# 64 keys by 64 queries in a half of TensorE's columns, in place of 128 by 128, for a gated recurrence's products

## The chip, the core and the metric

The kernel runs on one core of a Trainium2 chip. The metric is the device time of one execution in microseconds (us). The engines are TensorE (PE, with its weight loads, PEld, shown apart), VectorE (DVE), ScalarE (ACT), GpSimd (POOL) and SyncE (SP), which here only issues DMAs.

## What is computed

One layer of a decoder trunk for 256 tokens of width 2048, in fp32. A normalised input is multiplied by a wide matrix (12288 columns); its columns feed a short convolution (branch A), a gated linear recurrence (branch B) and merge gates. Both branches are projected back, merged and added, and a second gated term and a last normalisation follow. The change lies in branch B:

```python
def step(state, inp):
    qn, kn, vn, fn = inp
    b = jnp.cumsum(fn, axis=2)
    ...
    diff = b[:, :, :, None, :] - b[:, :, None, :, :]
    decay = jnp.exp(jnp.where(causal, diff, 0.0)) * causal_f
    a = jnp.einsum('bhtk,bhtsk,bhsk->bhts', qn, decay, kn)
    o = inter + jnp.einsum('bhts,bhsv->bhtv', a, vn)
```

Each of 8 heads has 128 features. `a[t, s]` couples a query at token t with a key at an earlier token s, and the decay between the two depends on the feature, so it can't be taken out of the sum over features as one factor per pair of tokens.

## The kernel before

The 256 tokens are held as two blocks of 128; the second is stored in reverse order, so that both blocks meet at their last rows. Products with weight matrices run in `product` (L859 to L864): each fp32 weight chunk and each activation is split into a high and a low part (float32r; `split`, L113 to L128, makes `whi` on ACT at L124 and `wlo` on DVE at L125), and three products per tile (high by high, high by low, low by high) are summed in PSUM banks named `g`. The main loop (L867 to L943) takes one weight chunk of 256 rows by 512 columns per step: 12 records of 512 columns on PE. Chunks are split three steps ahead (`LEAD`, L149), with four buffers for each part.

The work that follows each product is a generator: the main loop calls `advance()` once per step, and each generator then issues its work up to its next `yield`. So the order of each engine's instructions is fixed by the program: a generator's work is laid between the projections' products, a piece per step.

The recurrence is `hgrn(j)` (L341 to L514), run for j = 0 and 1, four heads each, called from `ep_og` (L333). It forms the 128 by 128 matrix a of each block and head without a loop over tokens:

- For each level size B in 128, 64, 32, 16, 8, 4 (`LEVELS`, L31), tokens of the later half of a group of B are coupled with those of its earlier half. The decay of such a pair factors at the boundary between the halves, so `level(B)` (L393) scales keys and queries with exponentials into a tile X, for which DVE and POOL each do two of the four parts (`combine`, L378), and `products(X)` (L355) multiplies for each head all 128 keys with all 128 queries. Of the first block X takes the keys of the earlier halves and the queries of the later ones, of the second (reversed) block the others, so that one product serves both blocks.
- Of each product only the couplings of this level are kept: `keep` (L362) copies, on DVE, through a mask from PSUM into the tile `both`, which collects all levels (L425). Then `both` is divided over the two blocks' matrices `a[:, 0]` and `a[:, 1]` through masks (L460).
- The pairs of two neighbouring tokens and the diagonal itself come from one product per block and head (L466 to L470), whose results are kept through masks as well (L474).
- The coupling of the second block's queries with the first block's keys is one whole product per head (`bo = products(X)`, L453), copied to `aoff` (L462).
- Last, a and aoff are multiplied with the values (L479 to L481).

The products of the recurrence are plain fp32, into PSUM banks named `s`, four of which take turns. A product of one group of four heads fills one bank.

Of the kernel before, what the change touches and what calls it, by code (L numbers as in the profile page):

```python
# [15 lines left out]
P = 128  # L16
T = 256
# [13 lines left out]
LEVELS = [128, 64, 32, 16, 8, 4]  # L31
# [13 lines left out]
def hybrid_kernel(ctx, tc, xT, x, pT, prm, gfin, masks, w_in, w_a, w_b, w_o, w_pg, w_pp, out):  # L45
    nc = tc.nc
# [27 lines left out]
    def nm(s):  # L74
        uid[0] += 1
        return f"{s}_{uid[0]}"

    def t4(tag="t4", bufs=None):
        bufs = bufs or {"tmp1": 8, "tmp2": 5, "tmp3": 5}[state["tmp"]]
        return pools[state["tmp"]].tile([P, 1024], F32, tag=tag, bufs=bufs, name=nm(tag))  # L80

    def bank(tag):
        return ps.tile([P, CW], F32, tag=tag, bufs=4, name=nm(tag))
# [87 lines left out]
    mask_t = const.tile([P, len(LEVELS) + 4, P], mybir.dt.int32, name="mask_t")  # L171
# [35 lines left out]
    def spread(ap, t):  # L207

        return ap.rearrange("p (b c t e) -> p t c b e", b=4, c=4, t=NT)[:, t]
# [120 lines left out]
    def ep_og(j, psum):  # L333
        sg, o = t4(), t4("og", 1)
        sig(psum, sg)
        times(psum, sg, o)
        state["og", j] = o
        yield
        yield from hgrn(j)

    def hgrn(j):  # L341
# [5 lines left out]
        kT, qT, b, tot, v, og = (state[n, j] for n in ("kT", "qT", "b", "tot", "v", "og"))  # L347
        tmp = pools["tmp1"]
        a = tmp.tile([P, 2, 4, P], F32, tag="a", bufs=1, name=nm("a"))
        nc.gpsimd.memset(a, 0.0)  # L350
        both = tmp.tile([P, 4, P], F32, tag="both", bufs=1, name=nm("both"))
        nc.gpsimd.memset(both, 0.0)
        aoff = tmp.tile([P, 4, P], F32, tag="aoff", bufs=1, name=nm("aoff"))

        def products(X):  # L355
            bk = bank("s")
            for h in range(4):
                s = slice(h * P, (h + 1) * P)
                nc.tensor.matmul(bk[:, s], X[:, 0, h, :], X[:, 1, h, :], start=True, stop=True)  # L359
            return bk  # L360

        def keep(dst, mask, src):  # L362
            nc.vector.copy_predicated(
                out=dst, mask=mask_t[:, mask : mask + 1, :].to_broadcast([P, 4, P]), data=src
            )

        def heads(ap):
            return ap.rearrange("p (h t) -> p h t", h=4)

        def halves(ap, B):  # L370
            r = ap.rearrange("p (n two h) -> p n two h", two=2, h=B // 2)
            return r[:, :, 0, :], r[:, :, 1, :]

        def tiles(ap, B):

            return ap.rearrange("p (h k n two c) -> p h k n two c", h=4, k=2, two=2, c=B // 2)
# [16 lines left out]
        def level(B):  # L393

            n, h = 1024 // B, B // 2
            e = t4()
            bl, br = halves(b, B)
            el, er = halves(e, B)
            if B > SCAN:
                nc.scalar.activation(out=el, in_=halves(y, B)[0], func=AF.Exp, scale=-1.0)  # L400
                nc.scalar.activation(out=er, in_=br, func=AF.Exp)  # L401
            else:
                ref = bl[:, :, h - 1 : h].to_broadcast([P, n, h])
                nc.vector.tensor_tensor(out=el, in0=bl, in1=ref, op=ALU.subtract)
                nc.gpsimd.tensor_tensor(out=er, in0=br, in1=ref, op=ALU.subtract)  # L405
                nc.scalar.activation(out=el, in_=el, func=AF.Exp, scale=-1.0)
                nc.scalar.activation(out=er, in_=er, func=AF.Exp)
            return combine(e, B)
# [4 lines left out]
            out=y.rearrange("p (n c) -> p n c", c=SCAN), in0=b.rearrange("p (n c) -> p n c", c=SCAN),  # L413
# [3 lines left out]
        X = level(LEVELS[0])  # L417
        yield
        yield
        for i in range(len(LEVELS)):  # L420
            nxt = level(LEVELS[i + 1]) if i + 1 < len(LEVELS) else None
            bk = products(X)
            yield
            yield
            keep(both, i, heads(bk))  # L425
            yield
            X = nxt

# [4 lines left out]
            out=el, in0=yl,  # L433
# [4 lines left out]
        X = t4("X", 2).rearrange("p (w h t) -> p w h t", w=2, h=4)  # L438
# [7 lines left out]
            out=f.rearrange("p (n c) -> p n c", c=1), in0=br, in1=bl, op=ALU.subtract  # L446
# [3 lines left out]
        yield  # L450
        nc.vector.reciprocal(out=rf[:, 256:], in_=f[:, 256:])
        yield
        bo = products(X)  # L453
        k2, q2 = tiles(kT, 2), tiles(qT, 2)
        fv, rv = (z.rearrange("p (h k n) -> p h k n", h=4, k=2) for z in (f, rf))
        for blk in range(2):
            kk, qq = k2[:, :, blk, :, 1 - blk, 0], q2[:, :, blk, :, 1 - blk, 0]
            nc.vector.tensor_tensor(out=kk, in0=kk, in1=rv[:, :, blk], op=ALU.mult)
            nc.gpsimd.tensor_tensor(out=qq, in0=qq, in1=fv[:, :, blk], op=ALU.mult)
            keep(a[:, blk], len(LEVELS) + blk, both)  # L460
        yield
        nc.vector.tensor_copy(out=aoff.rearrange("p h t -> p (h t)"), in_=bo)  # L462
        yield
        bk = [bank("s") for _ in range(2)]
        for blk in range(2):
            for h in range(4):  # L466
                s = slice(h * T + blk * P, h * T + (blk + 1) * P)
                nc.tensor.matmul(  # L468
                    bk[blk][:, h * P : (h + 1) * P], kT[:, s], qT[:, s], start=True, stop=True
                )  # L470
        yield
        yield
        for blk in range(2):
            keep(a[:, blk], len(LEVELS) + 2 + blk, heads(bk[blk]))  # L474
        yield
        o = [bank("s") for _ in range(2)]
        for h in range(4):
# [9 lines left out]
        for n in range(8):  # L487
            t, h = n // 4, n % 4
            if n == 4:
                yield  # L490
            nc.scalar.activation(
                out=sq[:, n * P : (n + 1) * P], in_=o[t][:, h * P : (h + 1) * P], func=AF.Square,
                scale=state["rstd1"][:, t : t + 1], accum_out=ss[:, n : n + 1],
            )
        for t in range(NT):
            s = slice(t * CW, (t + 1) * CW)
# [4 lines left out]
        for n in range(8):  # L501
            t, h = n // 4, n % 4
            if n == 4:
                yield
            nc.scalar.activation(
                out=spread(sq, t)[:, h], in_=yb[:, n * P : (n + 1) * P].rearrange("p (b e) -> p b e", e=32),
# [3 lines left out]
        for i in range(4):  # L510
            k = j * 4 + i
# [355 lines left out]
    for pos, (gi, c) in enumerate(steps[:last_group]):  # L867
# [36 lines left out]
        for i in range(2):  # L904
            k = 2 * c + i
            s = slice(i * CW, (i + 1) * CW)
# [41 lines left out]
    for t, halves in ((0, (0, 1)), (1, (0,)), (1, (1,))):  # L948
        bk, n = bank("g"), CW // 2
        for c in range(nlast):  # L950
# [4 lines left out]
            for i in range(2):  # L955
                k = 2 * c + i
                s = slice(i * CW + halves[0] * n, i * CW + (halves[-1] + 1) * n)
# [83 lines left out]
```

## Time and profile before

| | us |
|---|---|
| three runs | 833.39, 833.5, 833.75 (median 833.5) |
| the profiled execution | 834.5 |
| its span in the profile | 832.7 |
| PE busy in it | 821.6 |
| DVE busy | 530.0 |
| ACT busy | 433.0 |
| POOL busy | 92.4 |

The span is the time from the first to the last instruction of the profiled execution; 1.8 us lie around it. Busy time is the time in which an engine works on an instruction. Matmuls are pipelined, so that one record on PE begins before the one in front of it has ended; the distance between two starts is what one of them costs. An fp32 product of the recurrence stands as two records of PE (112 records for the 56 products of L359), a float32r product as one. In the groups of the profile, `s<-X` means that a tile or bank s is written from X; `128*128 128x128` are the array's rows and columns in use and the partitions and elements of the operands. The recurrences lie at 113 to 196 us (j = 0) and 298 to 381 us (j = 1).

### The profile page before, as it was taken

How to read it: one execution, taken by the hardware profiler on the slowest of the kernel's cores; microseconds unless marked ns; L12 is line 12 of the kernel's file. 1: busy time of each engine (PE TensorE's matmuls, PEld its weight loads, DVE VectorE, ACT ScalarE, POOL GpSimd, SP SyncE). 2: the span in 40 equal slices, each digit the busy share in tenths (PEclk: the TensorE clock that was granted, in tenths of full speed). 3: DMA queues.
4: the chain of work that ended last, by engine and by line, in shares of the span. 5: the costliest groups of instructions: out<-in, count | busy, mean ns of one | idle time of the engine just before them, and what ended most of it. 6: DMA issues, size and time to landing. Idle time of an engine off the chain costs nothing.

```text
span 832.7 us, 9822 instructions
## 1 busy us (share of the span) xinstructions
PE 821.6 (99%) x3754; PEld 682.6 (82%) x3754; DVE 530.0 (64%) x602; ACT 433.0 (52%) x561; POOL 92.4 (11%) x76
## 2 busy tenths in 40 slices
PE   9999999999999999999999999999999999999995
PEld 6788888888888888888888888888888888888885
DVE  6747578696776488696745545544644656679732
ACT  7666465455565465456544444444444455566523
POOL 1000035121000045110001000100100100001210
PEclk9999999999999999999999999999999999999998
DMA  9979555746777545646755765755665687887702
GB/s 326 389 274 332 195 196 168 232 148 190 279 251 249 202 164 191 205 166 195 283 179 185 253 202 203 243 179 192 244 203 202 230 293 276 285 302 284 299 1 102
DMA packets 40657, 187.20 MB, mean 225 GB/s; under 512 B 4641, under 2 KB 13857, under 8 KB 22433
## 3 DMA queue, kind: packets, MB, share of 16 engines
q1 hardware_dynamic: 40176, 185.78, 64.0%
q10 hardware_dynamic: 432, 0.79, 0.3%
q8 instruction: 29, 0.48, 0.2%
q14 instruction: 20, 0.16, 0.1%
HBM read 172.92 MB, written 13.63 MB: 224 GB/s over the span
## 4 chain that ended last, share of the span: by engine, by line
PE 93%; DMA 2%; ACT 2%; issue 2%; SPq 0%; DVE 0%; POOLq 0%; POOL 0%; ACTq 0%
PE g L864 91%; PE s L359 1%; DMA raw<-in_w_in 1%; DMA raw<-in_w_pp 1%; ACT t L643 0%; ACT whi L124 0%; PE s L468 0%; ACT xh L187 0%; PE s L481 0%; PE s L480 0%; PE s L479 0%; SPq L111 0%; ACT xs L698 0%; DVE wlo L125 0%; ACT t L681 0%
## 5 line engine op out<-in xcount | busy, mean ns | idle before, releaser
L125 DVE TENSOR_TENSOR wlo<-raw,whi 128x1024 fp32r<-128x1024 f32 (+1 forms) x293 | 361.1, 1237 | 261.7 <-ACT whi L124 259.8
L124 ACT ACTIVATE whi<-raw 128x1024 fp32r<-128x1024 f32 (+1 forms) x293 | 307.9, 1056 | 346.1 <-PE g L864 297.6
L864 PE MATMUL g<-wlo,xh 128*128 128x512 f32 (+1 forms) x912 | 351.6, 386 | 0.5 <-DVE wlo L125 0.5
L864 PE MATMUL g<-whi,xh 128*128 128x512 f32 (+1 forms) x912 | 351.4, 387 | 0.1
L864 PE MATMUL g<-whi,xl 128*128 128x512 f32 (+1 forms) x912 | 351.5, 385 | 0.0
L864 PEld LDWEIGHTS g<-wlo,xh 128*128 128x128 f32 x912 | 171.4, 188 | 34.7 <-DVE wlo L125 1.1
L864 PEld LDWEIGHTS g<-whi,xl 128*128 128x128 f32 x912 | 171.4, 188 | 34.2
L864 PEld LDWEIGHTS g<-whi,xh 128*128 128x128 f32 x912 | 171.4, 188 | 34.2 <-ACT whi L124 0.5
L864 PE MATMUL g<-wlo,mh 128*128 128x512 f32 x128 | 49.6, 389 | 0.0
L864 PE MATMUL g<-whi,mh 128*128 128x512 f32 x128 | 49.5, 389 | 0.0
L864 PE MATMUL g<-whi,ml 128*128 128x512 f32 x128 | 49.5, 389 | 0.0
L604 POOL TENSOR_TENSOR t<-ga,gb 128x512 f32<-128x512 f32 x8 | 14.1, 1788 | 249.1 <-DVE gb L600 249.1
L864 PE MATMUL g<-whi,yaTh 128*128 128x512 f32 x72 | 27.8, 391 | 0.8 <-ACT whi L124 0.8
L864 PE MATMUL g<-wlo,yaTh 128*128 128x512 f32 x72 | 28.2, 394 | 0.0
L864 PEld LDWEIGHTS g<-whi,mh 128*128 128x128 f32 x128 | 24.0, 188 | 5.0
L864 PEld LDWEIGHTS g<-whi,ml 128*128 128x128 f32 x128 | 24.0, 188 | 5.0
L864 PEld LDWEIGHTS g<-wlo,mh 128*128 128x128 f32 x128 | 24.0, 188 | 4.9
L864 PE MATMUL g<-whi,yaTl 128*128 128x512 f32 x72 | 27.9, 389 | 0.0
L405 POOL TENSOR_TENSOR t<-b 128x512 f32<-128x512 f32 x10 | 20.9, 2087 | 62.4 <-DVE b L309 33.6
L387 POOL TENSOR_TENSOR X<-t,kT 128x256 f32<-128x256 f32 x12 | 14.1, 1177 | 105.0 <-ACT t L401 63.4
L864 PE MATMUL g<-whi,ybTh 128*128 128x512 f32 x64 | 24.9, 389 | 0.0
L864 PE MATMUL g<-wlo,ybTh 128*128 128x512 f32 x64 | 24.9, 389 | 0.0
(149 smaller groups left out, 547.5 us busy)
## 6 DMA issues: line engine op xcount, KB each, us to landing
raw<-in_w_in SPq DMA_DIRECT2D x93, 1024.0 KB, 4.9
raw<-in_w_o SPq DMA_DIRECT2D x16, 1024.0 KB, 5.8
raw<-in_w_pg SPq DMA_DIRECT2D x16, 1024.0 KB, 5.5
turn<-t SPq DMA_DIRECT2D x72, 128.0 KB, 2.7
t<-turn SPq DMA_DIRECT2D x18, 512.0 KB, 4.7
raw<-in_w_a SPq DMA_DIRECT2D x8, 1024.0 KB, 5.0
raw<-in_w_b SPq DMA_DIRECT2D x8, 1024.0 KB, 5.0
raw<-in_w_in SPq DMA_DIRECT2D x6, 512.0 KB, 7.3
```

The lines of the kernel that those rows point to most:

```text
L124: a = nc.scalar.activation(out=hi[:, s], in_=src[:, s], func=AF.Copy)
L125: v = nc.vector.tensor_tensor(out=lo[:, s], in0=src[:, s], in1=hi[:, s].bitcast(F32), op=ALU.subtract)
L359: nc.tensor.matmul(bk[:, s], X[:, 0, h, :], X[:, 1, h, :], start=True, stop=True)
L387: eng.tensor_tensor(out=xv[:, w, :, :, half, :], in0=ev[:, :, blk, :, half, :], in1=src[:, :, blk, :, half, :], op=ALU.mult,)
L405: nc.gpsimd.tensor_tensor(out=er, in0=br, in1=ref, op=ALU.subtract)
L604: nc.gpsimd.tensor_tensor(out=spread(m, t), in0=blocks(ga[:, s]), in1=blocks(gb[:, s]), op=ALU.add)
L864: nc.tensor.matmul(psum, a, b, start=first and n == 0, stop=last and n == 2)
```

## The change

The level products and the diagonal's products are cut into quarters of 64 keys by 64 queries, and only two of the four are computed: at level 128 the keys of one half with the queries of the other, at the smaller levels and the diagonal each half with itself. The masks of the other two quarters are empty. `quarters` lists the two; r is the half of the keys, which are the rows of the result and the columns of TensorE's array, and c that of the queries. `tile_position` places the product in columns 0 to 63 or 64 to 127 of the array. The built instruction has an array tile of 128 rows by 64 columns there, and 128 by 128 everywhere else. `keep` copies the two quarters with one instruction each, of 64 partitions by 4 heads by 64 queries. The off-diagonal product (`bo`) and the copies of `both` into `a` stay whole; they are written out where `products` and `keep` stood.

```diff
-        def products(X):
-            bk = bank("s")
-            for h in range(4):
-                s = slice(h * P, (h + 1) * P)
-                nc.tensor.matmul(bk[:, s], X[:, 0, h, :], X[:, 1, h, :], start=True, stop=True)
-            return bk
-
-        def keep(dst, mask, src):
-            nc.vector.copy_predicated(
-                out=dst, mask=mask_t[:, mask : mask + 1, :].to_broadcast([P, 4, P]), data=src
-            )
...
+        def quarters(B):
+
+            n = P // 2
+            for r in range(2):
+                c = 1 - r if B == P else r
+                yield slice(r * n, (r + 1) * n), slice(c * n, (c + 1) * n)
+
+        def products(bk, key, query, B):
+
+            for h in range(4):
+                for r, c in quarters(B):
+                    nc.tensor.matmul(
+                        heads(bk)[r, h, c], key(h)[:, r], query(h)[:, c], start=True, stop=True,
+                        tile_position=(0, r.start),
+                    )
+
+        def keep(dst, mask, src, B):
+            for r, c in quarters(B):
+                nc.vector.copy_predicated(
+                    out=dst[r, :, c], mask=mask_t[r, mask : mask + 1, c].to_broadcast([P // 2, 4, P // 2]),
+                    data=src[r, :, c],
+                )
...
-            bk = products(X)
+            bk = bank("s")
+            products(bk, lambda h: X[:, 0, h, :], lambda h: X[:, 1, h, :], LEVELS[i])
...
-            keep(both, i, heads(bk))
+            keep(both, i, heads(bk), LEVELS[i])
...
         for blk in range(2):
-            for h in range(4):
-                s = slice(h * T + blk * P, h * T + (blk + 1) * P)
-                nc.tensor.matmul(
-                    bk[blk][:, h * P : (h + 1) * P], kT[:, s], qT[:, s], start=True, stop=True
-                )
+            kk, qq = (z.rearrange("p (h k t) -> p h k t", h=4, k=2)[:, :, blk, :] for z in (kT, qT))
+            products(bk[blk], lambda h: kk[:, h, :], lambda h: qq[:, h, :], 2)
```

More of the change, by code (lines that the diff above doesn't have):

```diff
@@ L452, in hgrn @@
         yield
-        bo = products(X)
+        bo = bank("s")
+        for h in range(4):
+            nc.tensor.matmul(heads(bo)[:, h, :], X[:, 0, h, :], X[:, 1, h, :], start=True, stop=True)
         k2, q2 = tiles(kT, 2), tiles(qT, 2)
@@ L459, in hgrn @@
             nc.gpsimd.tensor_tensor(out=qq, in0=qq, in1=fv[:, :, blk], op=ALU.mult)
-            keep(a[:, blk], len(LEVELS) + blk, both)
+            nc.vector.copy_predicated(
+                out=a[:, blk],
+                mask=mask_t[:, len(LEVELS) + blk : len(LEVELS) + blk + 1, :].to_broadcast([P, 4, P]), data=both,
+            )
         yield
@@ L473, in hgrn @@
         for blk in range(2):
-            keep(a[:, blk], len(LEVELS) + 2 + blk, heads(bk[blk]))
+            keep(a[:, blk], len(LEVELS) + 2 + blk, heads(bk[blk]), 2)
         yield
```

## The prediction

> **What bounds the kernel now.** I read the page first: the busy shares, the slices, and the chain that ended last.
>
> ```profile
> PE 821.6 (99%) x3754; PEld 682.6 (82%) x3754; DVE 530.0 (64%) x602; ACT 433.0 (52%) x561; POOL 92.4 (11%) x76
> PEclk9999999999999999999999999999999999999998
> PE 93%; DMA 2%; ACT 2%; issue 2%; SPq 0%; DVE 0%; POOLq 0%; POOL 0%; ACTq 0%
> ```
>
> TensorE (PE) is busy from end to end at a full granted clock, and 93% of the chain is its own work. A busy PE need not be one at its peak, so the next view is the list of what PE waited for in the whole run:
>
> ```profile
> PE s L744 <- DVE warm L740: 1.2, 1, 1.2
> PE g L864 <- ACT whi L124: 0.8, 1, 0.8
> PE g L864 <- DVE wlo L125: 0.5, 1, 0.5
> ```
>
> That is 2.5 us, all at the start: in the stretch 113 to 381 us, where both recurrences lie, the same view is empty. So there PE's own instruction stream sets the end, and what a product costs on PE reaches the end at full price. The chain in order of time gives that price:
>
> ```profile
> 116.48 0.89 PE s L359 x8
> 117.37 8.18 PE g L864 x36
> 125.54 0.89 PE s L359 x8
> ...
> 182.66 1.78 PE s L468 x16
> 184.45 8.18 PE g L864 x36
> ```
>
> A group of four products (one per head) is eight records and 0.89 us: each fp32 product runs as two records. One record is 0.89/8 = 0.111 us (1.78/16 for the diagonal's group gives the same). A record of the projections (512 columns) is 8.18/36 = 0.227 us. The durations are longer than these distances:
>
> ```profile
> L359 PE MATMUL s<-X 128*128 128x128 f32 x112 | 14.7, 274 | 0.0
> L864 PE MATMUL g<-whi,xh 128*128 128x256 f32 x32 | 9.1, 283 | 0.0
> ```
>
> A product's record lasts 0.274 us although the next starts after 0.111, so 0.163 us of it is a tail that overlaps the next one (projections: 0.386 less 0.227, 0.16). Keep this tail in mind.
>
> **The change part by part.** The order of instructions on each engine differs in 16 places on PE and 16 on VectorE (DVE), and nowhere on ScalarE, GpSimd or the DMA queues. Nothing moves.
>
> *Products, removed.* Six levels by four heads by two column groups j are 48 products, the diagonal's 2 by 4 by 2 are 16: 64 products, 128 records by 0.1113 us = 14.25 us. (The other 16 of the 112 records of L359 are the off-diagonal product, which stays whole.)
>
> *Products, added.* 128 products of 64 keys by 64 queries, so 256 records. No row has this shape, so the price of one is bounded. Above: 0.111 us, as now, if a record's price doesn't depend on its columns. Below: 0.029 us, half of a halved record, if the two halves of the array work side by side. Between: the price goes with the columns. The last projection runs at 256 columns with records 0.119 us apart (820.83, 820.95, 821.07 in the timeline), against 0.227 at 512; so 256 columns cost 0.108 us and what is fixed is some 0.011 us. The fp32 record at 128 columns takes 0.111, which is what 256 of those columns take, so I count each fp32 column twice: 64 columns fewer are 0.054 us less, and a record is 0.057 us (0.061 if the fixed 0.011 is in it too). I take 0.057, the value that the two rows of different width give: 256 by 0.0572 = 14.64 us, or **+0.4 us** against the 14.25 removed. In other words, twice as many instructions of half the length, one after the other, gain nothing.
>
> *Switching the array's division.* Every product of before runs on the whole 128 by 128 array. Now PE goes into 64-column halves and back around each of the 6 levels and the diagonal, for each j: 14 stays, 28 switches. No row shows a switch. Its price is at least nothing (if the division is only a label of the instruction), and at most what an empty array costs: the tail of 0.163 us twice per stay, and each time the weight load that is now hidden: it would stand open for about one record, 0.057 going in and 0.111 going out. That is 0.49 us a stay, 14 by 0.49 = 6.9 us. I take the tail alone, the nearest row, for a division that can't be changed under a product still in the array: 28 by 0.163 = **+4.6 us**.
>
> The Trainium skill ("TensorEngine Tiling (Array Packing)", section "Tiling Modes") says that changing the tiling mode drains TensorE. It gives no price, and no run so far shows one; by that rule this term stands, without it the sum below would be +0.4.
>
> *The masked copies on DVE.* Each of 16 copies becomes two of 64 partitions by 256 elements.
>
> ```profile
> L363 DVE COPY_PREDICATED both<-mask_t,s 128x512 f32<-128x512 int32 x12 | 8.8, 736 | 0.0
> L616 DVE TENSOR_TENSOR xs<-xs,g 128x512 f32<-128x512 f32 x8 | 5.1, 681 | 0.0
> L677 DVE TENSOR_TENSOR t<-t,pw 128x256 f32<-128x256 f32 x4 | 1.6, 425 | 15.3 <-ACT t L676 15.3
> ```
>
> The last two rows: halving the elements takes 0.256 us off, so a half copy is 0.736 - 0.256 = 0.48 us and a pair 0.22 us more than now. Bounds: nothing more (two exact halves) and 0.74 us more (no shorter for being half). Over 16 pairs 0 to 11.8 us, I take 3.5. At the path it costs **nothing**: in 113 to 196 us DVE is busy 67.2 of 83 us, so the eight pairs there have 15.8 us of idle time for 1.7 (at worst 5.9). Queued behind a copy is the weights' low part (wlo, L125), which PE waits for. It is made three chunks of 2.7 us ahead of its use, and DVE itself waits there for ScalarE, which waits for PE to release a buffer. Without that lead the 3.5 us would count. The order with its waits also shows DVE waiting for its own earlier copy once more per pair, and the second product of a first level with a wait on DVE that the first had before; both fall to work done a round earlier, so I cost them at nothing within the same idle time.
>
> *Sum.* The profiled execution took 834.5 us (span 832.7 and 1.8 around it), 1.0 above the median of 833.5. 834.5 + 0.4 + 4.6 = 839.5; less the 1.0 that this execution lies above the median, **838.5**.
>
> **The rivals**, all against the median.
>
> *Side by side (faster).* The two products of a head lie in different halves of the array. If a record in one half may run beside a record in the other, the second record of each product overlaps the first of the next: 16 records fit in 9 slots of 0.0572 = 0.515 us, the diagonal's 32 in 17 = 0.97. Together 12 by 0.515 + 2 by 0.97 = 8.1 instead of 14.25 us, a gain of 6.1. Switches at my price leave 832.0, at nothing 827.4, at the upper bound 834.3; it turns at 0.22 us a switch. For it: neighbouring products write different columns of the array and different partitions of a bank, and DVE has slack for a faster PE. Against it: in the timeline each weight load begins within 0.01 us of the start of the product before it (112.92 behind 112.91) and never earlier, so loads come one at a time, and a queue that takes load, product, load, product in turn pairs nothing.
>
> The same page of the Trainium skill, same section, says that tiles operate independently and that different tiles can load weights and multiply in parallel; "TensorE: Matmul & The Clock Gate", section "Measured speedup vs the span model", has 2.38 times for three column tiles. By these this rival is the outcome; no run here shows it yet.
>
> *A fixed price per record (much slower).* If load and product can't follow each other faster than the 0.111 us seen now, 256 records are 28.5 us: +14.25, and with switches +18.9: 852.4. From 0.056 us a record upward (14.25/256) it costs, whatever a switch does. For it: no two records in the trace start closer than 0.108 us. Against: the 256-column row shows the price falling with the columns.
>
> *Free switches, in turn.* +0.4: 833.9, nothing to be measured.
>
> **How the numbers follow.** What differs by under 0.2% (1.7 us) can hardly be told from no change here. In turn with paid switches: 0.45, its own range 836 to 842 (a switch from 0.1 us to the upper bound, a record of 0.057 to 0.061). Side by side: 0.30, of which 0.20 faster and 0.10 within 0.2%. Fixed price: 0.15. Free switches: 0.10. Faster 0.20, same 0.20, slower 0.60. The range runs from 828, side by side with nearly free switches, to 845, which is a record of 0.073 us with switches at the upper bound; it leaves out the fixed price and a little of the first rival.
>
> **What would show it.** In the chain the level's group stands as 0.89 us: near 0.9 again with the neighbouring projection groups grown, or a gap before and after it, is my case; 0.5 is side by side; 1.8 is the fixed price. A switch shows as the distance from the last projection record to the first product, 0.23 us now, and from the last product to the second projection record behind it. The granted clock must stay full, and PE's waits for wlo in 113 to 381 us must stay absent; if they appear, the DVE term was wrong.

## The result, and the profile after

Fourteen runs of the changed kernel have a median of 831.6 us (831.28 to 832.42), fourteen of the kernel before beside them 833.46. The ratio is 0.9977, with a 95% interval of 0.9970 to 0.9984: 1.9 us faster, where 838.5 and slower were forecast. The profiled execution took 831.59 us, with a span of 829.8. One execution of e1 below took 920 us at a granted clock of 0.85, against 0.996 to 0.998 in the others, and is left out of its time.

The page of the changed kernel, its lines on the engines, the clock and the chain:

```profile
PE 819.8 (99%) x3882; PEld 676.3 (81%) x3882; DVE 533.5 (64%) x618; ACT 433.4 (52%) x561; POOL 92.3 (11%) x76
PEclk9999999999999999999999999999999999999998
PE 94%; DMA 2%; issue 2%; ACT 1%; SPq 0%; DVE 0%; POOLq 0%; POOL 0%; ACTq 0%
```

PE has 128 records more and is busy for less time, at the same clock; DVE is busy for 3.5 us more. PE is still what sets the end. Its chain in order of time, the view that carried the price of a group before (start, length, what):

```profile
115.36 0.62 PE s L369 x16
115.97 8.38 PE g L878 x36
124.36 0.62 PE s L369 x16
124.97 8.38 PE g L878 x36
...
181.14 1.08 PE s L369 x32
182.22 8.39 PE g L878 x36
```

Sixteen records of a level now take 0.62 us where eight took 0.89 (the rival "side by side" had named 0.5), and the diagonal's 32 take 1.08 where 16 took 1.78. But the 36 projection records behind each group take 8.38 instead of 8.18. So the whole period counts, from group to group: 9.00 us (115.36 to 124.36) against 9.06 (116.48 to 125.54). The level groups gain 0.06 us each, the two diagonal groups 0.5.

Where the 0.2 us went is seen in PE's timeline around a group, first before, then after:

```profile
116.09 0.39 PE L864 MATMUL g<-whi,xl 128*128 128x512 f32 x1
116.32 1.05 PE L359 MATMUL s<-X 128*128 128x128 f32 x8
117.12 0.48 PE L864 MATMUL g<-whi,xh 128*128 128x512 f32 x1
117.44 0.40 PE L864 MATMUL g<-wlo,xh 128*128 128x512 f32 x1
```

```profile
114.97 0.39 PE L878 MATMUL g<-whi,xl 128*128 128x512 f32 x1
115.29 0.69 PE L369 MATMUL s<-X 128*64 128x64 f32 x16
115.90 0.50 PE L878 MATMUL g<-whi,xh 128*128 128x512 f32 x1
116.24 0.39 PE L878 MATMUL g<-wlo,xh 128*128 128x512 f32 x1
```

From the last projection record to the first product lie 0.32 us, where there were 0.23. Behind the group, a long first projection record is nothing new (0.50, before 0.48). What is new is when it starts: 0.15 us behind the start of the last product's record (115.750 to 115.902), where it was 0.03 (117.092 to 117.123). These 0.12 us, the shorter length of a half record (0.222 against 0.275, and the chain counts from its end) and some 0.03 us spread over the projection records that follow make up the 0.2. The list of waits names the entry: the first weight load of a group waits for nothing that the profile shows.

```profile
PEld s L369 <- issue: 4.6, 13, 0.4
PEld g L878 <- DVE wlo L125: 1.3, 3, 0.6
```

Thirteen times some 0.35 us; the same wait of the fourteenth stay in the halves stands in the list under POOL, with 0.4. Before there was no such line. Waits for wlo in the recurrence did not appear: the three of the second row lie outside 113 to 381 us.

Inside the 16 records the starts, read one by one from the trace, are these (us, the first level group):

```
115.287 115.293 | 115.393 115.400 | 115.452 115.458 | 115.510 115.517
115.567 115.575 | 115.627 115.633 | 115.685 115.692 | 115.743 115.750
```

They come in pairs 0.007 us apart, and the pairs 0.058 apart but for the first two, 0.106. The two first records both last 0.270 us and the others 0.222, as if each were the first of a stream of its own. That is the rival "side by side": two records per slot of 0.058, 0.029 us each. The trace doesn't name a record's half; that a pair is one of each has to come from the experiments.

The theory for the experiments: **the two halves of the array work beside each other, and each stay in them costs a fixed price for entering and leaving.** Rivals: a half-size record is cheap by itself, whatever lies beside it; the gaps belong to the products and not to the switch.

### The profile page after: what moved, and what is told of

The parts are those of the page before. It is cut to its first block, busy times and chain, and to the rows that moved or that the text cites. A ratio compares the mean times of both kernels' runs of the same rounds, so it can differ in the third digit from the quotient of the medians.

```text
span 829.8 us, 10094 instructions
## 1 busy us (share of the span) xinstructions
PE 819.8 (99%) x3882; PEld 676.3 (81%) x3882; DVE 533.5 (64%) x618; ACT 433.4 (52%) x561; POOL 92.3 (11%) x76
## 4 chain that ended last, share of the span: by engine, by line
PE 94%; DMA 2%; issue 2%; ACT 1%; SPq 0%; DVE 0%; POOLq 0%; POOL 0%; ACTq 0%
PE g L878 91%; DMA raw<-in_w_in 1%; PE s L369 1%; DMA raw<-in_w_pp 1%; ACT t L657 0%; ACT whi L124 0%; ACT xh L187 0%; PE s L495 0%; PE s L494 0%; PE s L493 0%; PE s L467 0%; ACT xs L712 0%; SPq L111 0%; DVE wlo L125 0%; ACT t L695 0%
```

## The experiments

Each ran beside the kernel before on the same chip, so times are compared through their ratios to it. The time of the kernel before was 833.5 to 833.9 us on these chips. The ratio is taken over all executions; it can differ from the quotient of the two medians in the fourth digit.

### One half after the other (e1, e5)

```diff
-            for h in range(4):
-                for r, c in quarters(B):
+            for r, c in quarters(B):
+                for h in range(4):
```

> The same products in the same tiles, but all four heads of the first half of the array before those of the second half, so neighbours share a half. Theory (two neighbours in different halves run side by side, a pair of records per 0.058 us; each stay in the halves costs 0.34 us on top): of a level's 16 records only the one place where the half changes can pair, so some 15 slots of 0.058 instead of 8 - the inner part of a stay grows from 0.46 to 0.87 us, the diagonal's from 0.93 to 1.62; 12 x 0.41 + 2 x 0.69 = +6.3 on 831.6, 837.9 us. Rival (a 64-column record is cheap by itself, 0.029 us, whatever its neighbour): 831.6. Third (the two halves have queues of their own, so that the second half's records overtake): 831.6 too, but the trace then shows records of both halves beside each other.

Measured: 836.53 us beside 833.82, ratio 1.0031 (1.0020 to 1.0042). None of the three readings had this time. e5 is the same kernel, for a trace at a granted clock of 0.997:

> The kernel of e1 once more, for a trace at the full granted clock (that of e1 fell to 0.85). Theory with strictly ordered records: inner part of a level's stay 0.87 us, no record of the second half before the eighth of the first. Third reading (each half has a queue of its own, filled in program order and of limited depth): the second half's first record starts beside the fifth or sixth of the first, inner part some 0.75 us, the diagonal's 1.35.

Measured: 836.09 us, a single execution. The chain of e5 shows the group:

```profile
115.64 0.90 PE s L369 x16
116.54 8.39 PE g L878 x36
```

The same instructions with the same switches, in another order: 0.90 instead of 0.62 us a group, and the whole gain is gone. So a half-size record isn't cheap by itself; that rival is out, and so is a strict order, which had 0.87 us inside a stay. The starts in e5 also show how far the overlap reaches:

```
115.574 115.680 115.739 115.797 115.855 | 115.861 | 115.914 115.968 115.972 116.026
116.030 116.085 116.143 116.201 116.260 116.318
```

The records of one half are 0.058 us apart, so the pairs 0.007 apart in the changed kernel are one of each half. At 115.861 a record begins whose length is that of a first one (0.271), beside the fifth of the half that runs; two streams of 0.058 then run beside each other until the first has had its eight. The ninth record in program order thus overtook three. This is the third reading as it was restated ahead of e5 (without a limited depth it had 831.6 for e1): each half takes its records in order, and the second half is reached past a few waiting records of the first, not past seven. The inner part was 0.744 us, as that reading expected.

### Blocks of two heads (e9)

```diff
-            for h in range(4):
+            for pair in ((0, 1), (2, 3)):
                 for r, c in quarters(B):
...
+                    for h in pair:
...
```

> As the changed kernel, but two heads of the first half, two of the second, two of the first, two of the second. In e5 the ninth record in program order, the first of its half, started beside the fifth, so it overtook three. Theory (each half takes its records in order, and a half can be reached past some three waiting records of the other): blocks of four records are just within reach, so the halves overlap nearly all the time, inner part of a level's stay 0.46 to 0.53 us, 831.6 to 832.5 us. Rival (only strict alternation by product pairs): as e5, 0.74 us inside, 836.

Measured: 832.84 us beside 833.86, ratio 0.9986 (0.9977 to 0.9995); inner part 0.511 us, and in the chain of this kernel:

```profile
115.32 0.66 PE s L370 x16
```

Four records of a half in a row cost 0.04 us a group against strict turns, and most of the overlap stays. So the order need not alternate product by product, but it can't be far from it.

### Which side of a record sets its price (e2)

```diff
-            products(bk, lambda h: X[:, 0, h, :], lambda h: X[:, 1, h, :], LEVELS[i])
+            for h in range(4):
+                for c in (slice(0, P // 2), slice(P // 2, P)):
+                    nc.tensor.matmul(heads(bk)[:, h, c], X[:, 0, h, :], X[:, 1, h, c], start=True, stop=True)
...
```

> The kernel before, whole array, but every level and diagonal product is cut into two of 128 keys by 64 queries (all four quarters are computed again, copies as before): twice the records, no halves, no switches. It measures a record whose streamed side alone is halved. By the prediction's step (a record's price goes with its streamed columns) 0.057 us a record, 833.9 us in all. By the rival of a price that the 128-column weight load sets: 0.107 to 0.111 us a record, +14 us, 847 to 848.

Measured: 848.78 us, ratio 1.0178 (1.0164 to 1.0192). By form, and in the chain:

```profile
L436 PE MATMUL s<-X 128*128 128x64 f32 x192 | 22.7, 271 | 0.0
```

```profile
116.55 1.73 PE s L436 x16
118.28 8.26 PE g L887 x36
```

The chain's 1.73 us leaves out what moved into the projection records behind the group (8.26 instead of 8.18). The starts within a group give the price: behind the first two they lie 0.112 us apart (116.556, 116.668, 116.780), just as the whole products' do (116.534, 116.646, 116.757 before), though only 64 columns are streamed. So with 128 keys as weights a narrower streamed side brings nothing; with 64 keys in a half the price is 0.058 (e5). The granted clock was 0.998 and 0.997. The weights' side has to be narrower too; whether that alone, 64 keys with 128 queries, would be as cheap was not measured.

### Twice as many stays (e3)

```diff
...
-            products(bk, lambda h: X[:, 0, h, :], lambda h: X[:, 1, h, :], LEVELS[i])
+            products(bk, lambda h: X[:, 0, h, :], lambda h: X[:, 1, h, :], LEVELS[i], (0, 1))
             yield
+            products(bk, lambda h: X[:, 0, h, :], lambda h: X[:, 1, h, :], LEVELS[i], (2, 3))
             yield
```

> As the changed kernel, but heads 0 and 1 of a level are multiplied in one step and heads 2 and 3 in the next, so that PE goes into the halves twice per level: 12 stays more with the same records. Theory (a stay costs 0.34 us whatever is in it): 12 x 0.34 = +4.1, 835.7 us, each stay with 8 records in some 0.23 us inside. Rival (the gaps around the group belong to the products, not to entering and leaving): 831.6.

Measured: 836.28 us beside 833.82, ratio 1.0033 (1.0020 to 1.0045).

```profile
115.46 0.38 PE s L369 x8
115.84 2.94 PE g L879 x12
118.78 0.38 PE s L369 x8
119.17 5.67 PE g L879 x24
124.83 0.38 PE s L369 x8
```

The period is 124.83 - 115.46 = 9.37 instead of 9.00 us with the same records: a stay more costs 0.37 us. Twelve are 4.4, and the ratio went from 0.9977 to 1.0033, 4.7 us, where the rival (the gaps belong to the products) had no change. The list of waits has 26 entries, as many as there now are stays:

```profile
PEld s L369 <- issue: 9.2, 26, 0.4
```

### Fewer stays (e4, e6, e7)

The products of two levels are multiplied together:

```diff
         for i in range(len(LEVELS)):
-            nxt = level(LEVELS[i + 1]) if i + 1 < len(LEVELS) else None
-            bk = bank("s")
-            products(bk, lambda h: X[:, 0, h, :], lambda h: X[:, 1, h, :], LEVELS[i])
+            held.append((i, X))
+            done_ = []
+            if len(held) == 2:
+                for k, x in held:
+                    bk = bank("s")
+                    products(bk, lambda h: x[:, 0, h, :], lambda h: x[:, 1, h, :], LEVELS[k])
+                    done_.append((k, bk))
+                held = []
+            nxt = level(LEVELS[i + 1]) if i + 1 < len(LEVELS) else None
...
```

> As the changed kernel, but the products of two neighbouring levels are multiplied together, in 3 stays per j instead of 6 (the next level's X is then scaled after them, since X has two buffers): 6 stays fewer. Theory: -6 x 0.34 = -2.0, 829.6 us. Rival (entering and leaving is not what costs): 831.6. Risk named ahead: DVE now waits for the group before it scales the next X; if wlo comes late for PE, up to 3 us come back and PE's waits for DVE show it.

Measured: 831.02 us beside 833.82, ratio 0.9964 (0.9951 to 0.9978): by the ratios 1.1 us less than the changed kernel, and by the spans of the two profiled executions 0.6 (829.8 and 829.2), where 2.0 were expected. The risk named was the wrong one. PE's list of waits:

```profile
PE s L475 <- POOL X L461: 0.9, 2, 0.4
PE g L886 <- DVE wlo L125: 0.4, 1, 0.4
```

Not wlo but the off-diagonal product waits, for GpSimd's part of its X. In the changed kernel that part ends only 0.29 us before it is used:

```profile
171.66 2.69 POOL L453 TENSOR_TENSOR X<-t,qT 128x512 f32<-128x512 f32 x1 [18.64 <-ACT t L448]
...
174.64 1.05 PE L467 MATMUL s<-X 128*128 128x128 f32 x8
```

The first row is GpSimd's timeline, the second PE's. A PE that comes 1 us earlier has to wait: with the weight load behind it, the two off-diagonal groups of e4 began 0.60 us late each. So that product was moved back by one `yield`:

> e4 with the off-diagonal product one step later, so that PE no longer arrives before GpSimd's part of its X: in e4 the six stays saved gave 2.1 us by the trace and two waits of PE for that X took 1.4 back. Theory: both waits gone and the whole 2.1 us gained on the changed kernel, 829.5 us. Rival (the merged stays have a second cost that the trace of e4 hides): no better than e4, about 831.

Measured: 829.54 us beside 833.5, ratio 0.9952 (0.9938 to 0.9965); the wait is gone, and the rival with it. Last, three levels a stay (the same with 3 in place of 2, three buffers of X, seven general ones):

> Three levels per stay, 2 stays per j for the levels instead of 6, the off-diagonal product one step later as in e6; X gets a third buffer, taken from the eight of the general work tiles (seven left). Theory: 8 stays fewer, 8 x 0.35 = -2.8 on 831.6, 828.8 us. Rival: with seven work tiles or three levels scaled in a row, ScalarE or DVE come late for wlo, PE waits for them, and it is no better than e6.

Measured: 828.60 us beside 833.5, ratio 0.9942 (0.9929 to 0.9954), the fastest of all. Its chain:

```profile
131.67 1.55 PE s L369 x48
133.22 24.70 PE g L887 x108
157.93 1.55 PE s L369 x48
```

Three levels take 157.93 - 131.67 = 26.26 us, where three periods of the changed kernel are 27.00: 0.74 for two stays fewer, 0.37 each again (in e6 two levels take 17.63 us instead of 18.00). With 26 stays (e3), 14 (changed), 8 (e6) and 6 (e7) the ratios fall by 0.39, 0.35 and 0.42 us a stay. Their intervals are wide, but they agree with the traces: the time goes with the number of stays.

### The parts alone (e8, e10, e11)

> The kernel before with the masked copies alone in halves, the products whole. By the prediction's step (3.5 us more on DVE, all beside PE) 833.5 us, within 0.2% of before. Rival (DVE's copies delay wlo or a bank's release): slower by up to 3.5 us, with PE's waits for wlo in the recurrence.

Measured: 833.5 us beside 833.5, ratio 0.9999 (0.9990 to 1.0007). The copies on DVE cost nothing on the path. In the changed kernel a half copy lasts

```profile
L376 DVE COPY_PREDICATED both<-mask_t,s 64x256 f32<-64x256 int32 x24 | 10.7, 445 | 0.6
```

so a pair is 2 x 0.445 - 0.736 = 0.15 us longer than the whole one.

> Only the diagonal's products and copies are halved, the levels stay whole: 2 stays of 32 records. Stay price by the traces: 0.348 us + 0.0291 a record, against 0.1117 a whole record: 1.281 instead of 1.789, twice: -1.0, 832.5 us. Rival (in turn, as predicted): +0.05 + 2 x 0.33 = +0.7, 834.2.

Measured: 832.5 us beside 833.86, ratio 0.9989 (0.9980 to 0.9998).

> Only the levels' products and copies are halved, the diagonal stays whole: 12 stays of 16 records, 0.815 instead of 0.896 us each: -1.0, 832.5 us. Rival (in turn, as predicted): +0.3 + 12 x 0.33 = +4.3, 837.8.

Measured: 833.05 us beside 833.86, ratio 0.9989 (0.9980 to 0.9998). The two intervals are nearly as wide as the effects, so it is the traces that divide the gain: 2 x 0.5 us for 2 stays of the diagonal, 12 x 0.06 for 12 stays of the levels. Each part alone is faster than before and not slower, which the forecast's sizes (834.2 and 837.8) would have had.

## Why the prediction was wrong

- **What bounds the kernel**: right. PE's stream set the end before and after, and changes of it came through, but for e4, where a new wait of PE took part of one back.
- **Products, removed (14.25 us)**: right.
- **Products, added (14.64 us)**: this is the step that failed, "twice as many instructions of half the length, one after the other, gain nothing". They don't run one after the other: 256 records at 0.029 are 7.4 us, 7.2 less than the sum had. The price of a record alone was right (0.057 forecast, 0.058 in e5), though by luck in its reason: the 256-column row speaks of the streamed side, and e2 shows that this side alone brings nothing. The argument against the rival was a view read too far: that each weight load begins behind the product before it was seen with one undivided array and says nothing of two halves. Nor did it show that loads come one at a time: within a group of whole products they lasted 0.19 us and began 0.11 apart.
- **Switches (4.6 us)**: right in kind, a little small. 0.33 us a stay forecast, 0.37 measured (e3, e7), 14 stays 5.2 us. That the tail gave this size is luck in part: not 0.163 us lie open on either side, but some 0.09 at the entry (0.32 less 0.23) and 0.23 at the exit (0.15 + 0.34, less a half record of 0.03 and a projection record of 0.23), the rest in the slower first pair and the projection records behind.
- The Trainium skill ("TensorEngine Tiling (Array Packing)", section "Tiling Modes") said both: that a change of mode drains TensorE and that tiles work in parallel. The traces agree with the second, with 0.058 us a pair. For the first they show a price, 0.37 us a stay, but not that TensorE had run empty: the first half record starts 0.32 us behind a projection record whose modelled length is 0.39. The forecast took the first rule's result and gave the second 0.30.
- **Copies on DVE (3.5 us, nothing on the path)**: right on the path: e8 shows no effect. The copies took 16 x 0.15 = 2.5 us more; that DVE's whole busy time rose by just 3.5 is chance.
- **The sum** with the failed step put right: 833.5 - 14.25 + 7.4 + 5.2 = 831.9, against 831.6 measured. The rival "side by side" had 832.0 with the switches at the price taken.
- **A fixed price per record**: out for halves, but e2 shows where it holds (0.112 us with 128 keys), and its time: 848.8. What spoke for it was misread: behind each group of whole products the first projection record starts 0.03 us after the last product's (117.092 to 117.123), so some starts were closer than 0.108.

## What to carry to other kernels

Column halves of TensorE paid here when neighbouring products lay in different halves; then two records, each with 64 columns of weights and 64 streamed, shared a slot. Narrowing the streamed side alone gained nothing. Entering and leaving cost 0.37 us, and a whole fp32 record turned into two halves saves 0.112 - 0.058 = 0.054, so a stay has to replace seven whole records before it gains (eight gained 0.06 us, sixteen 0.5; four, in e3, lost 0.15). Collect such products into few long stays, and when PE gets faster by it, look for the operand that was just in time.

## What was not expected of the hardware

- Records in different halves don't keep program order among each other. It follows from the starts and lengths of records, as the trace doesn't name their half: in the changed kernel the second product of a head starts 0.007 us behind the first record of the first one, ahead of its second; in e5 a half's first record overtook three of the other half, and blocks of four (e9) still overlapped most of the time.
- Leaving the halves costs more than entering them, some 0.23 against 0.09 us. Why, and why the projection records behind a stay run a few hundredths of a us late in all, stays open.
